# Grouped-query attention heads: the keys' low parts laid down twice, so that both score passes have 128 rows

## The chip, the core and the metric

The kernel runs on one core of a Trainium2 chip. The metric is the device time of one execution in microseconds (us). Five engines work side by side, each through its own queue in order: PE (TensorE, matrix products; the loading of its weights is shown apart as PEld), DVE (VectorE), ACT (ScalarE), POOL (GpSimd) and SP, which here issues transfers. An engine that needs another's result waits on a semaphore.

## What is computed

Two transformer blocks in float32 follow each other. The first has retention, neighbourhood attention, memory attention and a mixture of experts. The second has two layers over 512 latent tokens and 256 context tokens; each layer has three kinds of attention heads, side by side, and a feed-forward part. Cut to the heads that the change touches:

```python
q_g = _rope_2(_rms(gq.reshape(B, T, GQA_HEADS, GQA_DIM), g_gqa_q), rope_large)      # 8 heads of 64
k_g = _rope_2(_rms(gk.reshape(B, T, GQA_KV_HEADS, GQA_DIM), g_gqa_k), rope_large)   # 2 groups of keys
...
k_all = jnp.concatenate([k, kc], axis=2)          # 512 latent and 256 context keys
s = jnp.einsum('bhgqd,bhkd->bhgqk', q, k).astype(jnp.float32) * scale
p = jax.nn.softmax(s, axis=-1)
o = jnp.einsum('bhgqk,bhkd->bhgqd', p, v)
```

In layer 0 the context's 256 tokens are queries too, over the context's keys alone; in layer 1 only the 512 latents are.

## The kernel before, in words

PE takes its operands as float32r, a shortened float32. To keep the accuracy, a value is split in two such parts, high and low (`hi`, `lo`), and a product of two values is made of several products of parts that PE adds up in PSUM.

`attention` (L1759) makes a list of 20 units for a layer, one for each head or half head: 4 latent heads (`mla`), 8 differential ones (`diff`), 8 grouped-query ones (`gqa`, L1823; two groups of keys with four heads each). A unit has a preparation, a generator whose steps are run one at a time, and returns a list of passes: queries, keys, and the number of rows (features on partitions) that the product sums over.

- `mla` has three passes of 96 rows: high by high, high by low, low by high.
- `diff` lays its parts of 32 features one above the other and has one pass of 96 rows.
- `gqa` has queries of 128 rows, 64 high features above 64 low ones (`q1`). Its first pass takes them against `T1`, the high parts of the keys laid down twice (128 rows); the second takes the 64 high rows of the queries against `T2`, the low parts of the keys (64 rows). For the first head of a group the keys are prepared: `gk1` is written on DVE (L1830), `gk2` is the remainder, on POOL (L1831); both are turned on PE, six tiles of tokens each (`to_T`, L129), and copied from PSUM by ACT (L1734).

`pipeline` (L1867) runs the units one behind the other. While unit u's probabilities are turned (`turned`, PE at L131 into `tp`, then split in two parts by ACT, DVE and POOL: L1940 to L1942, L91, L92) and multiplied by the values (`products`, L1957, up to five tiles of keys later), unit u+1's scores are made (`scores`), and unit u+2 is prepared. For each tile of 128 queries `scores` runs the passes over 512 keys and then over 256 (`mms`, L1899):

```python
for j, (q, k, rows) in enumerate(passes):
    nc.tensor.matmul(p, q[:rows, qs], k[:rows, a:b], start=j == 0, stop=j == len(passes) - 1)
```

DVE takes the maximum of each row (L1905), ACT the exponential (L1908). There are two buffers in PSUM for scores (`sn`), three for turned tiles (`tp`). In layer 0 a head has four tiles of queries and then one step for the two context tiles, over 256 keys (L1913, L1919); in layer 1 it has four tiles.

What the differential heads still need, a norm over their outputs, stands behind the pipeline in the code (L1855 to L1860), but depends on their outputs alone; a scheduler orders each engine's work by what is ready and by its own estimates, and puts it among DVE's work of the grouped-query heads.

Of the kernel before, what the change touches and what calls it, by code (L numbers as in the profile page):

```python
# [8 lines left out]
F = mybir.dt.float32  # L9
# [14 lines left out]
# columns of the vector pack, in blocks of 128 features  # L24
# [8 lines left out]
# groups of 256 columns of the second block's input projection: name, first column  # L33
# [4 lines left out]
class Kern:  # L38
# [15 lines left out]
    def W(self, ap, n=2048, k=None, steps=1, pin=False, eng=None):  # L54
        """Weight chunk [128, n] of float32 from DRAM as an exact pair of float32r tiles."""
        key = ap.tensor.name, ap.offset
        if key in self.early:
            return self.early.pop(key)
        return self.pair(self.raw(ap, n), n, k, steps, pin, eng)

    def ahead(self, *chunks):
        """Loads weight chunks (name, index, k) before their use; W finds them then."""
# [10 lines left out]
    def pair(self, raw, n=2048, k=None, steps=1, pin=False, eng=None):  # L73
        """pin: not before what the engines have to do first, though it may seem ready."""
# [12 lines left out]
    def split(self, hi, lo, src, scale=None, bias=None):  # L87
        """hi + lo = src (times scale), both float32r."""
# [15 lines left out]
    def psum(self, mm, big=0, words=1024, own=()):  # L104
        """Banks of PSUM: mm of one bank, big of several."""
# [16 lines left out]
    def rows6(self, name, dtype=F):  # L122
        """[128, 6, 1024]: six tiles of rows, or what else takes their place."""
        return self.yp.tile([128, 6, 1024], dtype, name=name, tag="rows", bufs=1)
# [12 lines left out]
    def bcast_rows(self, ap, n, parts=128):  # L137
        """DRAM row of n elements seen by all partitions."""
        return bass.AP(tensor=ap.tensor, offset=ap.offset, ap=[[0, parts], [1, n]])

    def rinv(self, ss, n, count, eps, name):
        """1/sqrt(ss/count + eps) for a [128, n] tile: a first guess from the bits of the float, three Newton steps.
        With -r for the guess, (v r^2 - 3) r is 2 of the next one, and so on: -1, 2, -16, 8192 of them; v is 8192^2 of its own."""
# [33 lines left out]
    def transpose_rows(self, rows, nt, dst, evac):  # L177
        """rows: list of [128, 1024] tiles; evac(kt, t0, n, psum [128, n*128])."""
# [25 lines left out]
    # =====================================================================  # L204
# [30 lines left out]
    def b1_norm(self):  # L235
        """Loads the rows and the first weights; first_norm(t) and first_turn(t) then make the part of h of tile t."""
        nc = self.nc
        # products of nothing, that start the tensor engine's clock
# [36 lines left out]
    def first_norm(self, t):  # L275
        """Norms the row tiles from t on that share a step: 0, 1, or 2 and 3."""
# [23 lines left out]
    def w_in(self, g):  # L300
        """Columns 256*g.. of w_in, all of K."""
        return self.W(self.i["w_in"][g, 0], k=8)

    def proj_b(self, g, evac, after=lambda t: None, before=()):
        """Tokens on partitions: out[tok, 256 columns of group g]."""
# [12 lines left out]
    def proj_a(self, g, evac):  # L318
        """Columns on partitions: out[128 columns, 512 tokens]."""
# [17 lines left out]
    def retention(self):  # L337
# [6 lines left out]
        y = rp.tile([128, 4, 1024], F, name="y")              # [tok, tile, 4 heads of 256]  # L344
# [3 lines left out]
        def queries(c):  # L348
            """q and k of the heads 2c, 2c + 1: [128, hi or lo, head, tok]"""
# [34 lines left out]
        def scores(hd):  # L384
            # decay by the distance of the tokens: E[p, i - 128 j + 384] for tile j of the keys
# [15 lines left out]
        def outputs(hd):  # L401
# [4 lines left out]
            for i in range(4):  # L406
# [6 lines left out]
                # group norm over the head's 256 values  # L413
# [9 lines left out]
        # log sigmoid of the decays: min(x, 0) - log1p(exp(-|x|)), log1p by its atanh series  # L423
# [41 lines left out]
        # silu of the gate projection  # L465
# [21 lines left out]
    def branch_rows(self):  # L487
        """Where the rows of an attention branch are collected: [tok, tile, 512]."""
        return self.mix[:, 4:6].rearrange("p a (b c) -> p (a b) c", b=2)

    def branch_out(self, yT, nk, wname, gate_group, first=False, middle=lambda: None):
        """mix^T += sigmoid(gate^T) * (w^T y^T), features on partitions."""
        nc = self.nc
        nw = 2048 // nk                       # columns of w per chunk
# [1757 lines left out]
```

## Time and profile before

| | |
|---|---|
| median of three runs | 3059.8 us (3050.26 to 3065.61) |
| the profiled execution's span | 3055.9 us |
| PE busy in it | 2907.7 us (95%) |
| DVE busy | 1784.5 us (58%) |
| ACT busy | 1296.3 us (42%) |
| POOL busy | 483.3 us (16%) |
| grouped-query heads' scores, layer 0 | from 1408.2 us on |
| grouped-query heads' scores, layer 1 | up to 2589.0 us |

The profile is one execution, with the start, the length and the releaser of each instruction. PE is busy nearly throughout, but matmuls are pipelined, and the busy time of one includes what it waits for its weights. So the distance between the starts of two matmuls says more than their lengths. A line number stands for a line of the code above; a helper's line stands for all that call it.

### The profile page before, as it was taken

To read this page: it belongs to the slowest core of one execution; us is meant where nothing else is said; L and a number is where in the kernel's file an instruction comes from. 1 tells how busy PE (TensorE), PEld (TensorE's weight loads), DVE (VectorE), ACT (ScalarE), POOL (GpSimd) and SP (SyncE) were. 2 spreads that over 40 slices of the span, in tenths; PEclk is the share of its full clock that TensorE was granted. 3 is DMA by queue.
4 is the path that set the end of the run, shared out by engine and by line. 5 is a ranking of instruction groups with operands and counts; after the bars stand their busy time and mean duration, and the time that the engine had idled before them with its cause. 6 is when DMAs were issued, how large, how long until landed. Compare 5 with 4: busy or idle time off the path is not lost. (4 is left out here: it accounts for less than half of the span.)

```text
span 3055.9 us, 44719 instructions
## 1 busy us (share of the span) xinstructions
PE 2907.7 (95%) x17896; PEld 2473.1 (81%) x17896; DVE 1784.5 (58%) x3187; ACT 1296.3 (42%) x2275; POOL 483.3 (16%) x478
## 2 busy tenths in 40 slices
PE   8999999999899979899998999999898999899998
PEld 6997777679788869787688888888798776788887
DVE  6652254346688876788747242434665886644445
ACT  3232243324577754597645121211342876432222
POOL 2200010001110042255312000000310543100001
PEclk9999999999899989999999999999999999899999
DMA  5443464446799862510023121212143300322221
GB/s 197 153 140 138 143 234 152 183 155 242 267 392 378 312 225 75 179 27 19 1 90 128 59 71 54 78 48 83 62 138 98 96 20 1 125 110 96 97 97 69
DMA packets 130084, 399.78 MB, mean 131 GB/s; under 512 B 62199, under 2 KB 74887, under 8 KB 93128
## 3 DMA queue, kind: packets, MB, share of 16 engines
q1 hardware_dynamic: 116206, 350.04, 31.9%
q0 software_dynamic: 13520, 46.55, 4.6%
q8 instruction: 143, 2.34, 0.3%
q14 instruction: 71, 0.58, 0.1%
q10 hardware_dynamic: 144, 0.26, 0.0%
HBM read 356.64 MB, written 39.39 MB: 130 GB/s over the span
## 5 line engine op out<-in xcount | busy, mean ns | idle before, releaser
L82 DVE TENSOR_TENSOR wlo<-raw,whi 128x2048 fp32r<-128x2048 f32 (+2 forms) x195 | 419.3, 2153 | 280.2 <-ACT whi L81 279.7
L81 ACT ACTIVATE whi<-raw 128x2048 fp32r<-128x2048 f32 (+2 forms) x203 | 351.9, 1739 | 490.9 <-PE fd L101 132.2
L99 PE MATMUL fg<-hT,whi 128*128 128x512 f32 (+1 forms) x1120 | 389.1, 348 | 2.1 <-ACT hT L1374 2.1
L100 PE MATMUL fg<-hT,whi 128*128 128x512 f32 (+1 forms) x1120 | 389.7, 348 | 1.2 <-POOL hT L1376 1.2
L101 PE MATMUL fg<-hT,wlo 128*128 128x512 f32 (+1 forms) x1120 | 389.2, 348 | 0.0
L100 PEld LDWEIGHTS fg<-hT,whi 128*128 128x128 f32 x1120 | 213.7, 191 | 31.0 <-POOL hT L1376 1.7
L99 PEld LDWEIGHTS fg<-hT,whi 128*128 128x128 f32 x1120 | 212.1, 190 | 31.9 <-ACT hT L1374 2.5
L101 PEld LDWEIGHTS fg<-hT,wlo 128*128 128x128 f32 x1120 | 212.0, 189 | 29.0
L1942 POOL TENSOR_TENSOR pelo<-pe,pehi 128x512 fp32r<-128x512 f32 x140 | 180.7, 1292 | 233.5 <-DVE pehi L1941 227.1
L2104 DVE TENSOR_TENSOR sg<-sg,fg 128x512 f32<-128x512 f32 (+1 forms) x70 | 40.1, 572 | 295.0 <-PE fg L101 295.0
L101 PE MATMUL fd<-whi,hl 128*128 128x512 f32 x440 | 174.9, 397 | 0.0
L1905 DVE TENSOR_REDUCE smx<-sn 128x1 f32<-128x768 f32 x160 | 152.3, 952 | 38.2 <-PE sn L1899 37.7
L100 PE MATMUL fd<-wlo,hh 128*128 128x512 f32 x440 | 174.6, 397 | 0.0
L99 PE MATMUL fd<-whi,hh 128*128 128x512 f32 x440 | 174.1, 396 | 0.0
L2080 POOL TENSOR_TENSOR acc<-acc,gt 128x512 f32<-128x512 f32 x20 | 30.7, 1536 | 867.9 <-ACT sqj L164 867.9
L2075 DVE TENSOR_TENSOR acc<-acc,fd 128x512 f32<-128x512 f32 x180 | 120.7, 685 | 71.9 <-PE fd L101 71.9
L131 PE MATMUL tp<-ident,pn 128*128 128x128 f32 x960 | 151.8, 278 | 2.6 <-DVE pelo L92 1.8
L1908 ACT ACTIVATE pn<-sn,smx 128x768 f32<-128x768 f32 x160 | 143.5, 902 | 12.0 <-DVE smx L1905 6.8
L99 PE MATMUL eg<-whi,xt 128*96 128x256 f32 x512 | 146.5, 286 | 0.0
L100 PE MATMUL eg<-wlo,xt 128*96 128x256 f32 x512 | 144.6, 282 | 0.9 <-DVE wlo L82 0.9
L82 DVE TENSOR_TENSOR wlo<-rawx,whi 128x2048 fp32r<-128x2048 f32 x58 | 132.9, 2292 | 20.9 <-ACT whi L81 20.8
L101 PE MATMUL eg<-whi,xt 128*96 128x256 f32 x512 | 144.3, 282 | 0.0
(661 smaller groups left out, 7755.8 us busy)
## 6 DMA issues: line engine op xcount, KB each, us to landing
raw<-in_w_in SPq DMA_DIRECT2D x53, 1024.0 KB, 5.0
raw<-in_w_ada SPq DMA_DIRECT2D x48, 1024.0 KB, 5.1
raw<-in_f_gate SPq DMA_DIRECT2D x22, 1024.0 KB, 4.8
raw<-in_f_up SPq DMA_DIRECT2D x22, 1024.0 KB, 4.8
raw<-in_f_down SPq DMA_DIRECT2D x22, 1024.0 KB, 4.8
rawx<-in_e_gate SPq DMA_DIRECT2D x19, 1024.0 KB, 14.2
rawx<-in_e_up SPq DMA_DIRECT2D x19, 1024.0 KB, 8.9
rawx<-in_e_down SPq DMA_DIRECT2D x18, 1024.0 KB, 8.3
```

Of the source, the lines that this page charges most:

```text
L81: keep(nc.scalar.activation(hi[:, c], raw[:, c], AF.Copy))
L82: keep((eng or nc.vector).tensor_tensor(lo[:, c], raw[:, c], hi[:, c].bitcast(F), op=OP.subtract))
L99: t.matmul(ps, lh, rh, start=first, stop=False)
L100: t.matmul(ps, lh, rl, start=False, stop=False)
L101: t.matmul(ps, ll, rh, start=False, stop=last)
L131: self.nc.tensor.transpose(out, in_, self.ident[:k, :k])
L1905: nc.vector.tensor_reduce(m[:, t:t + 1], p[:, :768], axis=AX.X, op=OP.max, negate=True)
L1908: nc.scalar.activation(P[t], p[:, :768], AF.Exp, bias=m[:, t:t + 1], accum_out=su[:, t:t + 1])
L1942: nc.gpsimd.tensor_tensor(el, e, eh.bitcast(F), op=OP.subtract)
L2075: nc.vector.tensor_tensor(acc[:, t, cs], acc[:, t, cs], p, op=OP.add)
L2080: nc.gpsimd.tensor_tensor(acc[:, t, cs], acc[:, t, cs], gt[t // 4][:, cs], op=OP.mult)
L2104: nc.vector.tensor_tensor(sg, sg, pp[1], op=OP.mult)
```

## The change

The low parts of the keys are laid down twice, as the high ones already are: `gk2` becomes as wide as `gk1`, POOL makes the same subtraction a second time into its second half, the turning of `gk2` gives 128 rows and not 64, and the second pass takes all 128 rows of the queries, high and low, against it. The product of the two low parts, which was left out, comes into the scores by that.

```diff
-                k2 = ap.tile([128, 6, 64], R, name="gk2", tag="st", bufs=3)
+                k2 = ap.tile([128, 6, 2, 64], R, name="gk2", tag="st", bufs=3)
                 nc.vector.tensor_copy(k1, r[:, :, None, :].to_broadcast([128, 6, 2, 64]))
-                nc.gpsimd.tensor_tensor(k2, r, k1[:, :, 0].bitcast(F), op=OP.subtract)
+                nc.gpsimd.tensor_tensor(k2[:, :, 0], r, k1[:, :, 0].bitcast(F), op=OP.subtract)
+                nc.gpsimd.tensor_tensor(k2[:, :, 1], r, k1[:, :, 1].bitcast(F), op=OP.subtract)
                 yield
                 T1 = yield from self.to_T(ap, "gkT1", lambda t: k1[:, t].rearrange("p c d -> p (c d)"), 6, 128)
-                T2 = yield from self.to_T(ap, "gkT2", lambda t: k2[:, t], 6, 64)
+                T2 = yield from self.to_T(ap, "gkT2", lambda t: k2[:, t].rearrange("p c d -> p (c d)"), 6, 128)
...
-            return [(q1, T1, 128), (q1, T2, 64)], v
+            return [(q1, T1, 128), (q1, T2, 128)], v
```

The new file has no comments either, and its lines from L1832 on have numbers higher by one. The buffers of the tag `st` were already as large as `gk1`.

The order of the instructions on PE, DVE, ACT and SP is the same in both programs; on PE and ACT some have another size. On PE, where the keys of the first group of layer 0 are turned (`gk_14233` is `gk1`, `gk_14234` is `gk2`, `pn` the probabilities), before:

```order
L129 MATMUL tp<-identr,gk_14233 128x128 x2
L131 MATMUL tp<-ident,pn 128x128 x4
L1957 MATMUL pv<-pehi,vp 128x512
L1957 MATMUL pv<-pelo,vp 128x512
L129 MATMUL tp<-identr,gk_14234 64x128 x4
```

and after:

```order
L129 MATMUL tp<-identr,gk_14233 128x128 x2
L131 MATMUL tp<-ident,pn 128x128 x4
L1958 MATMUL pv<-pehi,vp 128x512
L1958 MATMUL pv<-pelo,vp 128x512
L129 MATMUL tp<-identr,gk_14234 128x128 x4
```

Nothing moved; the four turns give 128 rows.

On POOL, in the first group of layer 1 (`pelo` are the low parts of probabilities, `vp` the values, `gqst` the queries), before:

```order
L1721 TENSOR_TENSOR vp<-vr,vp 128x6x64
L1831 TENSOR_TENSOR gk_24040<-gkr,gk_24039 128x384
L1942 TENSOR_TENSOR pelo<-pe,pehi 128x512 x3
L1840 TENSOR_TENSOR gqst<-gqr,gqst 128x4x64
L1942 TENSOR_TENSOR pelo<-pe,pehi 128x512 x2
```

and after:

```order
L1721 TENSOR_TENSOR vp<-vr,vp 128x6x64
L1831 TENSOR_TENSOR gk_24042<-gkr,gk_24041 128x6x64
L1943 TENSOR_TENSOR pelo<-pe,pehi 128x512
L1832 TENSOR_TENSOR gk_24042<-gkr,gk_24041 128x6x64
L1943 TENSOR_TENSOR pelo<-pe,pehi 128x512 x2
L1841 TENSOR_TENSOR gqst<-gqr,gqst 128x4x64
L1943 TENSOR_TENSOR pelo<-pe,pehi 128x512 x2
```

The second subtraction stands behind one split of probabilities. In the other three groups it stands right behind the first one.

## Rows read from the trace of the kernel before

**Rows 1.** The page, its first part: busy us (share) and instructions of each engine.
```profile
PE 2907.7 (95%) x17896; PEld 2473.1 (81%) x17896; DVE 1784.5 (58%) x3187; ACT 1296.3 (42%) x2275; POOL 483.3 (16%) x478
```

**Rows 2.** Windows, differential heads, layer 0: length, busy us per engine (count), granted clock, DMA.
```profile
1359.10:1371.00 11.90, 11.06 (x80) 9.32 (x79) 11.32 (x20) 10.72 (x27) 6.40 (x6) 1.00 0.08 19
...
sum 95.60, PE 89.18 PEld 76.47 DVE 86.85 ACT 86.96 POOL 58.54; mean PE 11.15 PEld 9.56 DVE 10.86 ACT 10.87 POOL 7.32
```

**Rows 3.** Windows, grouped-query heads one, three, four and five of layer 0; sum of eight.
```profile
1408.30:1423.00 14.70, 14.70 (x81) 10.38 (x80) 11.45 (x18) 10.31 (x24) 6.14 (x5) 1.00 0.07 15
...
1438.50:1453.90 15.40, 15.35 (x84) 10.73 (x82) 13.56 (x27) 10.31 (x25) 6.29 (x5) 1.00 0.00 1
1453.90:1470.80 16.90, 16.68 (x96) 11.71 (x94) 15.27 (x30) 11.66 (x27) 7.50 (x7) 1.00 0.01 1
1470.80:1486.40 15.60, 15.49 (x84) 10.77 (x82) 12.76 (x20) 10.00 (x23) 6.82 (x6) 1.00 0.04 3
...
sum 124.30, PE 123.48 PEld 86.49 DVE 89.41 ACT 81.45 POOL 48.38; mean PE 15.44 PEld 10.81 DVE 11.18 ACT 10.18 POOL 6.05
```

**Rows 4.** Windows, grouped-query heads three, four and six of layer 1; sum of eight.
```profile
2514.10:2527.30 13.20, 12.95 (x65) 8.67 (x64) 11.05 (x25) 7.98 (x17) 4.56 (x4) 1.00 0.00 0
2527.30:2542.80 15.50, 14.92 (x82) 10.04 (x80) 13.25 (x28) 9.79 (x22) 5.44 (x5) 1.00 0.00 1
...
2554.80:2567.80 13.00, 12.68 (x66) 8.58 (x65) 7.65 (x13) 8.04 (x17) 3.82 (x3) 1.00 0.00 0
...
sum 102.70, PE 99.92 PEld 67.28 DVE 69.99 ACT 63.68 POOL 35.06; mean PE 12.49 PEld 8.41 DVE 8.75 ACT 7.96 POOL 4.38
```

**Rows 5.** The line L1899: idle us before its instructions, and how often.
```profile
  issue: 36.0, 128
```

**Rows 6.** Timeline of PE, a head of layer 0: start, us, what, count.
```profile
1423.00 1.45 PE L1899 MATMUL sn<-gkT,gqT 128*128 128x512 f32 x4
1424.38 0.66 PE L131 MATMUL tp<-ident,pn 128*128 128x128 f32 x4
1424.79 0.47 PE L1957 MATMUL pv<-pehi,vp 128*128 128x512 f32 x1
...
1434.95 1.29 PE L1899 MATMUL sn<-gkT,gqT 128*128 128x256 f32 x4
1436.18 0.66 PE L1970 MATMUL tp<-fold,oT 128*128 128x64 f32 x4
```

**Rows 7.** Timeline of PE's weight loads, a score tile; idle time and its cause in brackets.
```profile
1410.56 0.18 PEld L1899 LDWEIGHTS sn<-gkT,gqT 64*128 64x128 f32 x1 [0.24 <-issue]
1410.98 0.50 PEld L1899 LDWEIGHTS sn<-gkT,gqT 128*128 128x128 f32 x2 [0.24 <-issue]
```

**Rows 8.** Timeline of PE, a latent head of layer 0, three passes of 96 rows.
```profile
1282.29 0.60 PE L131 MATMUL tp<-ident,pn 128*128 128x128 f32 x4
1282.64 0.48 PE L1957 MATMUL pv<-pehi,vp 128*128 128x512 f32 x1
...
1283.19 0.40 PE L1899 MATMUL sn<-mhi 96*128 96x512 f32 x1
...
1283.90 0.28 PE L1899 MATMUL sn<-mhi 96*128 96x256 f32 x1
...
1284.25 0.60 PE L131 MATMUL tp<-ident,mqrow 128*96 128x128 f32 x4
```

**Rows 9.** Timeline of POOL, first group of keys, layer 0.
```profile
1387.70 0.99 POOL L1831 TENSOR_TENSOR gk<-gkr,gk 128x384 fp32r<-128x384 f32 x1
```

**Rows 10.** Timeline of PE, the same keys' low parts turned.
```profile
1399.78 0.40 PE L129 MATMUL tp<-identr,gk 128*64 128x128 f32 x4
```

**Rows 11.** Windows, behind the heads of layer 0; the granted clock is third from the end.
```profile
1548.00:1554.00 6.00, 5.69 (x26) 5.29 (x26) 1.98 (x4) 1.74 (x4) 0.00 (x0) 0.50 0.95 326
```

**Rows 12.** Timeline of PE there: matmuls of 256 columns.
```profile
1550.04 0.42 PE L100 MATMUL wo<-wlo,hT 128*128 128x256 f32 x1
1550.26 0.41 PE L99 MATMUL wo<-whi,hT 128*128 128x256 f32 x1
```

## The prediction, made before the changed kernel ran

> **What bounds the kernel now.** I read the page's engine sums first: the matmul engine (PE) is busy 95% of the span [rows 1], so time is saved where PE does less, or stands less. Its busy time counts time in which a matmul only waits for its weights, so I went on to the stretches that the change touches: per head of the second block, the busy time of each engine. In the grouped-query heads of both layers PE is at 97 to 99% of the window, and the next engine, VectorE (DVE), has 89.41 of 124.3 us and 69.99 of 102.7 [rows 3, 4]. In the differential heads just before them, whose scores take one pass, PE, DVE and ScalarE (ACT) are all at 91 to 93% [rows 2]. So here PE sets the pace; there nobody does alone.
>
> Then the line of the score matmuls, L1899: 36.0 us of idle time before its loads, 128 times, is put down to "issue": the weight loader waited for nothing that the profile shows [rows 5]. The timeline of the loader shows where: in a score tile the load of 64 rows comes 0.24 us after the load of 128 rows has ended, and the load of 128 rows after that again 0.24 us later [rows 7]. The latent and the differential heads have passes of one height, 96 rows, and no such gap stands in their timeline [rows 8].
>
> **The price of one tile.** A score tile is four matmuls: 128 rows by 512 keys, 64 by 512, 128 by 256, 64 by 256. From its start at 1423.00 to the next PE work at 1424.38 it takes 1.38 us [rows 6]. The latent heads show the same widths without a change of height: three passes of 96 rows over 512 and 256 keys, also begun behind a product with the values, run from 1283.19 to 1284.25, 1.06 us, or 0.353 a pass [rows 8]. Two passes are then 0.71. The tile gives back 1.38 - 0.71 = 0.67. The work behind it pays too: four turns take 1424.79 - 1424.38 = 0.41 behind a mixed tile [rows 6] and 1282.64 - 1282.29 = 0.35 behind even passes [rows 8]. That makes 0.73 a tile. The context's queries see 256 keys: two tiles of two passes take 1436.18 - 1434.95 = 1.23 [rows 6], against four of (1284.25 - 1283.90)/3 = 0.117 [rows 8], that is 0.47; with the 0.06 behind it, 0.82.
>
> **The sum on PE.** Layer 0 has 8 heads of 4 tiles and one such pair, layer 1 has 8 heads of 4 tiles: 64 x 0.73 + 8 x 0.82 = 46.7 + 6.6 = 53 us, or 53/288 = 0.185 for each of the 288 changes of height. A head of layer 0 gets 4 x 0.73 + 0.82 = 3.7 us shorter, one of layer 1 2.9. No matmul gets longer: the new pass streams as many columns, and 96 rows and 128 rows lie side by side in rows 8 (96-row scores, then turns of 128 rows) without a gap.
>
> **What is late next.** The order of every engine stays, but for the added subtraction, so the question is which engine can't follow. I take 3.7 or 2.9 from each head's window and hold DVE's busy time against the rest [rows 3, 4]. Layer 0: 14.7 leaves 11.0 for DVE's 11.45; 15.4 leaves 11.7 for 13.56; 16.9 leaves 13.2 for 15.27; 15.6 leaves 11.9 for 12.76. Over by 0.45 + 1.86 + 2.07 + 0.86 = 5.2 us. Layer 1: 13.2 leaves 10.3 for 11.05, 15.5 leaves 12.6 for 13.25: over by 1.4. (In these heads the end of the differential attention, L1855 to L1860, lies on DVE between the score maxima.) A DVE that never waits would thus hold back 6.6 us. It does wait: its fullest head among the differential ones in rows 2 has 11.32 of 11.9 us, 95%. On the 53.0 + 24.3 = 77.3 us of DVE work in these six heads 5% is another 4.1. Between 6.6 and 10.7 I take 9, nearer the upper end, because that head's work is the most alike. In the other ten heads DVE has room (7.65 of the 13.0 - 2.9 = 10.1 us left in a plain head of layer 1, and ACT 8.04 [rows 4]); I put 0.2 us each, 2 in all. A differential head, with all three engines near their limit, stands 11.95 us at 11.15 of PE's work [rows 2], so some waiting there is to be expected.
>
> **What is added.** Four subtractions on POOL (two groups of keys, two layers) at 0.99 us [rows 9], 4.0 us of POOL time. POOL is busy 48.38 of 124.3 us [rows 3], and the turns of the low keys come 12 us after the subtraction (from 1387.70 to 1399.78) [rows 9, 10]. In the first group of layer 1 the second subtraction comes behind one split of probabilities; the order shows it, the trace of before can't show the wait, and the same kind of cover stands before its use. Without that cover it would be at most 4 x 0.99 us on PE. Behind it on POOL stand splits of probabilities, whose products come five tiles later. What may show is DVE: work of DVE beside POOL can be slower. That lies between 0 and 4 us. The 24 turns of the low keys load 128 columns and not 64; half of a load's 0.18 us [rows 7] is 0.09 each, so between 0, where it lies beside the turn before, and 2 us. Of both together, 0 to 6, I take 1, as the cover of 12 us is long and rows 8 show loads beside matmuls. ACT's copy has more partitions and the same columns: nothing.
>
> So 53 - 9 - 2 - 1 = 41 us. The profiled execution spans 3055.9 us and the median of the three runs is 3059.8, 3.9 more; I carry the difference: 3055.9 - 41 + 3.9 = 3019.
>
> **A rule that speaks against it.** Even passes are begun every 0.117 us at 256 keys, though each has a load of its own, and a load of 128 columns takes 0.18 us even alone [rows 7, 8]: the load lies beside the matmul before it. The Trainium skill, page "TensorE: Matmul & The Clock Gate", section "Part 3: Packing small matmuls — row/col tiling", says that a weight load overlaps matmuls in flight only when it goes to another row group. By that rule two passes of full height would have their loads bare, and the widened pass would lose what overlap it had. The trace of this case doesn't agree, for passes of 96 rows; what the rule would do here is the first rival below.
>
> **Rivals.**
> - *Nothing gained* (3060). Two passes on the same rows get no load beside a matmul, so all four loads of a tile lie bare. Then a tile is 0.71 + 4 x 0.19 = 1.47 us, today's 1.38 or more. For it: "issue" names no cause. Against it: rows 8. 3%.
> - *PE's whole 53 us* (3007, and 3003 if a switch costs a little more than I read). The DVE work over the budget slips into the heads beside, which have room: 10.1 - 7.65 = 2.4 us in a plain head of layer 1 [rows 4]. For it: the excess is small. Against it: each engine keeps its order, and PE can be two score tiles ahead at most. 20%.
> - *DVE takes over more* (3029). DVE in the six full heads reaches only the 91% of the differential stretch (86.85 of 95.6): 77.3/0.91 = 85 against the 70.7 us that PE leaves, 14 lost, and the ten others lose 0.5 each, 5, with 3 us from POOL: 53 - 22 = 31. 15%.
> - *Slower: PE's clock.* With more waiting, PE could be granted the lower level in these stretches. At a granted 0.50 (1.2 of 2.4 GHz) a matmul of 256 columns begins every 0.22 us [rows 11, 12] and not every 0.117, 1.85 times as long. After the change the two stretches last some 174 us (124.3 + 102.7 - 53); the 41 us are gone, and 15 more lost, once 56/0.85 = 66 us of them run at that level: 3075 and over. For it: the level falls right after the heads [rows 11]. Against it: 1.00 in the differential head of rows 2, where PE already stands 0.84 of 11.90 us. 2%.
>
> **How the numbers follow.** My forecast 3019 has 60%. Its own span is 3011 to 3027; the range takes in the whole gain and the heavier DVE: 3003 to 3030. "Same" is within 0.5%, 15 us, about what a measurement of this kernel can tell from no change. Faster: forecast, whole gain and heavier DVE, 95%; same: nothing gained, 3%; slower 2%.
>
> **What would show it.** Right: L1899's grouped-query matmuls have one form of 128 rows, the idle time by "issue" before their loads is gone, a tile takes 0.7 to 0.8 us, the plain heads 11.6 to 12.0 us in layer 0 and 10.0 to 10.3 in layer 1, DVE is over 90% in the third to fifth head of layer 0, and PE's idle time names DVE or ACT. Wrong: gaps of 0.24 us stay between loads of one height; or heads are as long as before with PE waiting for DVE throughout; or the granted clock in these windows falls below 1.00.

## The result, and the profile after

The median goes from 3061.66 us (four runs, 3050.26 to 3065.61) to 3020.87 us (four runs, 3012.79 to 3027.51): 40.8 us less, a ratio of 0.9881 with a 95% interval of 0.9854 to 0.9908. The forecast was 3019, the gain 41.

The page's engine sums, which answer to [rows 1]; busy us, share of the span, instructions:

```profile
PE 2854.9 (95%) x17896; PEld 2464.6 (82%) x17896; DVE 1776.4 (59%) x3187; ACT 1294.7 (43%) x2275; POOL 487.9 (16%) x482
```

PE has 52.8 us less to do and is as full as before. The heads of layer 0, third, fourth, seventh and the sum of eight, against [rows 3]; length, busy us per engine (count), granted clock, DMA:

```profile
1439.30:1453.40 14.10, 12.04 (x84) 10.33 (x83) 13.76 (x26) 10.04 (x25) 6.43 (x5) 1.00 0.00 1
1453.40:1467.80 14.40, 13.04 (x97) 11.51 (x95) 14.26 (x31) 11.51 (x28) 7.84 (x7) 1.00 0.01 2
...
1493.60:1505.70 12.10, 12.05 (x84) 10.27 (x83) 8.57 (x15) 9.81 (x24) 5.13 (x4) 1.00 0.00 0
...
sum 103.60, PE 96.42 PEld 83.01 DVE 87.16 ACT 79.89 POOL 49.81; mean PE 12.05 PEld 10.38 DVE 10.89 ACT 9.99 POOL 6.23
```

The heads of layer 1, fourth, sixth and the sum, against [rows 4]:

```profile
2494.90:2509.00 14.10, 12.55 (x83) 9.93 (x81) 13.96 (x33) 9.71 (x22) 5.65 (x6) 1.00 0.01 1
...
2518.70:2529.00 10.30, 9.98 (x66) 8.27 (x65) 7.21 (x13) 7.87 (x16) 3.86 (x3) 1.00 0.00 0
...
sum 83.10, PE 79.12 PEld 65.54 DVE 67.58 ACT 62.95 POOL 36.47; mean PE 9.89 PEld 8.19 DVE 8.45 ACT 7.87 POOL 4.56
```

The 20.7 and 19.6 us are all here. In the plain heads PE is still at 95 to 100% of the window; in the third and fourth head of layer 0 and the fourth of layer 1 DVE has taken its place (98, 99 and 99%), and PE stands 1.4 to 2.1 us. In the first and fifth head of layer 0 PE is at 89% (11.28 of 12.70 us and 12.13 of 13.60).

The weight loads of the score matmuls (L1900 now), grouped by form: the 64-row group of before, then the one group of after; what stands behind the second bar is the idle time before them and its causes:

```profile
L1899 PEld LDWEIGHTS sn<-gkT,gqT 64*128 64x128 f32 x144 | 26.3, 183 | 30.7 <-issue 20.5
```

```profile
L1900 PEld LDWEIGHTS sn<-gkT,gqT 128*128 128x128 f32 x288 | 49.3, 188 | 18.1 <-ACT pn L1909 9.5 <-ACT gqT L1734 0.3
```

The line's grouped-query matmuls, and what ended the idle time before all its instructions, against [rows 5]:

```profile
L1900 PE MATMUL sn<-gkT,gqT x288: 277/286/505, 1414.2 to 2545.1; 128*128 128x256 f32 x80, 128*128 128x512 f32 x64
...
  ACT pn L1909: 29.7, 57
```

All 288 loads have 128 rows; before, 144 of them had 64. The row "issue: 36.0, 128" has gone from the list; ACT's exponential is now first in it (the 57 times cover all heads of the block). PE in the third head of layer 0, against [rows 6]; start, us, what, count, and idle time with its cause:

```profile
1439.28 0.86 PE L1900 MATMUL sn<-gkT,gqT 128*128 128x512 f32 x4
1439.98 0.60 PE L131 MATMUL tp<-ident,pn 128*128 128x128 f32 x4
1440.33 0.48 PE L1958 MATMUL pv<-pehi,vp 128*128 128x512 f32 x1
...
1444.09 0.66 PE L131 MATMUL tp<-ident,pn 128*128 128x128 f32 x4 [1.00 <-DVE pelo L92]
...
1449.66 0.72 PE L1900 MATMUL sn<-gkT,gqT 128*128 128x256 f32 x4
1450.22 0.39 PE L1958 MATMUL pv<-pehi,vp 128*128 128x512 f32 x1
```

A tile of scores takes 0.70 us (1439.28 to 1439.98; before 1.38), the four turns behind it 0.35 (before 0.41), the context's pair 0.56 (before 1.23). And PE waits 1.00 us for a low part that DVE has not yet made.

**Length of a head in every kernel that was run**, in us, from the start of its first score matmul to that of the next head's; "all" runs from the first score matmul of the eight heads to the first turn of the merged rows behind them. Each is read from one profiled execution, so these lengths leave out what varies elsewhere in the program. The experiments ran on three chips, on which the kernel before had medians of 3055.4 us (x1 to x4), 3058.9 (x5 to x7, after_again) and 3061.3 (x8, x9); across chips the ratio is to be compared.

| kernel | L0 third | fourth | fifth | seventh | L0 all | L1 fourth | seventh | L1 all | median, us | ratio to before (95%) |
|---|---|---|---|---|---|---|---|---|---|---|
| before | 15.40 | 16.93 | 15.56 | 15.48 | 139.5 | 15.49 | 12.93 | 117.6 | 3061.7 | |
| after | 14.08 | 14.44 | 13.56 | 12.14 | 118.9 | 14.11 | 10.32 | 97.9 | 3020.9 | 0.9881 (0.9854 to 0.9908) |
| x1_two_changes | 14.04 | 15.57 | 14.48 | 13.69 | 127.6 | 14.15 | 11.53 | 106.4 | 3030.1 | 0.9910 (0.9894 to 0.9926) |
| x2_preparation_alone | 15.40 | 17.06 | 15.56 | 15.48 | 139.7 | 15.60 | 12.93 | 117.7 | 3058.1 | 1.0011 (0.9995 to 1.0026) |
| x3_end_on_pool | 14.08 | 13.00 | 19.34 | 12.14 | 122.5 | 13.11 | 10.30 | 96.5 | 3018.1 | 0.9870 (0.9850 to 0.9891) |
| x4_end_left_out | 12.58 | 13.72 | 11.68 | 12.14 | 114.7 | 12.09 | 10.31 | 95.5 | 3018.1 | 0.9881 (0.9861 to 0.9901) |
| x5_latent_64 | 14.07 | 14.44 | 13.75 | 12.14 | 119.0 | 14.10 | 10.31 | 97.9 | 3056.8 | 0.9996 (0.9977 to 1.0014) |
| x6_pool_two_buffers | 14.07 | 12.99 | 12.01 | 12.13 | 115.8 | 13.08 | 10.31 | 96.5 | 3011.5 | 0.9847 (0.9817 to 0.9876) |
| x7_high_part_on_dve | 12.88 | 14.72 | 16.76 | 12.10 | 120.6 | 13.81 | 10.31 | 97.2 | 3016.0 | 0.9867 (0.9831 to 0.9904) |
| after_again | 14.07 | 14.45 | 13.59 | 12.13 | 118.9 | 14.09 | 10.32 | 97.9 | 3018.9 | 0.9865 (0.9834 to 0.9895) |
| x8_no_pool_split | 11.82 | 14.34 | 11.82 | 11.73 | 112.8 | 12.33 | 10.27 | 94.3 | 3004.1 | 0.9828 (0.9804 to 0.9852) |
| x9_both | 11.82 | 14.32 | 11.40 | 12.00 | 112.7 | 12.32 | 10.20 | 94.2 | 3010.9 | 0.9851 (0.9827 to 0.9875) |

From before to after the heads lose 20.7 + 19.7 = 40.4 us, what the medians lose (40.8). The latent and the differential heads have the same lengths in both, each within 0.1 us. The spans of the two profiled executions differ by more, 44.9 us; that is variation elsewhere (the experiment after_again).

### The profile page after: what moved, and what is told of

The parts are those of the page before. It is cut to its first block, busy times and chain, and to the rows that moved or that the text cites. A ratio compares the mean times of both kernels' runs of the same rounds, so it can differ in the third digit from the quotient of the medians.

```text
span 3011.0 us, 44725 instructions
## 1 busy us (share of the span) xinstructions
PE 2854.9 (95%) x17896; PEld 2464.6 (82%) x17896; DVE 1776.4 (59%) x3187; ACT 1294.7 (43%) x2275; POOL 487.9 (16%) x482
## 5 line engine op out<-in xcount | busy, mean ns | idle before, releaser
L1906 DVE TENSOR_REDUCE smx<-sn 128x1 f32<-128x768 f32 x160 | 151.7, 948 | 18.9 <-PE sn L1900 18.1
L2076 DVE TENSOR_TENSOR acc<-acc,fd 128x512 f32<-128x512 f32 x180 | 120.6, 685 | 68.2 <-PE fd L101 68.2
L1909 ACT ACTIVATE pn<-sn,smx 128x768 f32<-128x768 f32 x160 | 143.9, 904 | 19.6 <-DVE smx L1906 16.2
## 6 DMA issues: line engine op xcount, KB each, us to landing
rawx<-in_e_down SPq DMA_DIRECT2D x18, 1024.0 KB, 10.7
```

Source lines behind the costliest of these rows:

```text
L1906: nc.vector.tensor_reduce(m[:, t:t + 1], p[:, :768], axis=AX.X, op=OP.max, negate=True)
L1909: nc.scalar.activation(P[t], p[:, :768], AF.Exp, bias=m[:, t:t + 1], accum_out=su[:, t:t + 1])
L2076: nc.vector.tensor_tensor(acc[:, t, cs], acc[:, t, cs], p, op=OP.add)
```

## The experiments

**Half of the changes of height.** The kernel before, where every second group of passes runs in reverse order, so that two passes of 64 rows follow each other and a tile has two changes, not four:

```diff
-                for j, (q, k, rows) in enumerate(passes):
+                turn = turn and passes[0][2] != passes[-1][2]
+                for j, (q, k, rows) in enumerate(passes[::-1] if turn else passes):
...
-                mms(p[:, 512:768], t, 512, 768)
+                mms(p[:, 512:768], t, 512, 768, turn=True)
```

> The kernel before, with one edit: over the second keys of a score tile the 64-row pass comes first, so that the two 64-row passes lie side by side and a tile has two changes of height, not four (the context pair likewise). As many 64-row matmuls as before, nothing added on any other engine. Theory (each change of height costs 0.185 us): 144 of 288 changes are gone, 26.6 us of PE, and DVE's budget is kept or nearly kept in all heads; a score tile of 1.38 us takes 1.01, the eight heads of layer 0 take 124.3 - 15 = 109 us, of layer 1 102.7 - 12 = 91, the whole 25 us less than before (ratio 0.992). Rival (a 64-row pass is slow in itself, as its load never lies beside a matmul): 64-row passes are as many, so nothing is gained: tile 1.38, ratio 1.000. Second rival (the last 13 of the 53 us were never there, a change costs 0.14): 20 us, tile 1.10.

Measured: 25.2 us less than before on the same chip (3030.1 against 3055.4); the heads lose 12.0 and 11.2 us, less than the forecast 15 and 12; the third head of layer 0, for one, loses 1.36 of the 1.8 us that its ten changes are worth. The seventh head, where PE waits for other engines at most 0.3 us, loses 1.79 us for 10 changes in layer 0 and 1.40 for 8 in layer 1: 0.179 and 0.175 a change. The weight loader in the first tile of the seventh head of layer 0:

```profile
1501.14 0.19 PEld L1900 LDWEIGHTS sn<-gkT,gqT 128*128 128x128 f32 x1
1501.70 0.29 PEld L1900 LDWEIGHTS sn<-gkT,gqT 64*128 64x128 f32 x2 [0.36 <-issue]
1502.24 0.19 PEld L1900 LDWEIGHTS sn<-gkT,gqT 128*128 128x128 f32 x1 [0.25 <-issue]
1502.37 0.46 PEld L131 LDWEIGHTS tp<-ident,pn 128*128 128x128 f32 x4
```

The idle time by "issue" stands where the height changes, and only there: the second load of 64 rows follows the first without one. So the price is one of the change, not of the pass of 64 rows. The same passes, with the same work, were half as dear in another order.

**The wider low parts without the wider pass.**

```diff
-            return [(q1, T1, 128), (q1, T2, 128)], v
+            return [(q1, T1, 128), (q1, T2, 64)], v
```

> The changed kernel's preparation with the passes of before: the low parts are laid down twice and turned to 128 rows, but the second pass takes only the first 64. It measures what the change adds by itself. Theory: 1 us, bounds 0 to 6: heads of layer 0 at 124 to 126 us, of layer 1 at 103 to 104, ratio 1.000 to 1.002. Rival (the 12 us between PE's 53 and the 41 found are the price of the added work on POOL and beside it on DVE): 8 to 12 us, ratio 1.003 to 1.004, seen in the heads in which the keys are prepared (seven and eight of the differential, two and three of the grouped-query ones).

Measured: the heads are 0.23 us longer than before (0.14 + 0.09, all of it in the fourth head of each layer, where the second group's keys are prepared), and the differential heads, where the first group's are, have the lengths of before, each within 0.1 us; the ratio of the medians is 1.0011, and its interval takes in 1. The added subtractions and wider turns cost next to nothing.

**The end of the differential attention, left out or moved.** Between the score maxima of the grouped-query heads DVE also runs L1856 to L1861. x4 is the changed kernel without these lines; x3 has two of them on POOL:

```diff
-            nc.vector.tensor_tensor(y, y, r[:, t, :, None].to_broadcast([128, 4, 64]), op=OP.mult)
-            nc.vector.tensor_tensor(y, y, gd[:, None, :].to_broadcast([128, 4, 64]), op=OP.mult)
+            nc.gpsimd.tensor_tensor(y, y, r[:, t, :, None].to_broadcast([128, 4, 64]), op=OP.mult)
+            nc.gpsimd.tensor_tensor(y, y, gd[:, None, :].to_broadcast([128, 4, 64]), op=OP.mult)
```

> The changed kernel without the end of the differential attention (L1856 to L1861: the norm over the heads' outputs and its gain are left out of the computation). Theory: all of DVE's excess in the heads is gone; plain heads took 12.1 us in layer 0 and 10.3 in layer 1, so layer 0 takes 8 x 12.1 + 1 = 98 us (103.6 with it), layer 1 8 x 10.1 = 81 (83.1), together 7 to 8 us: this is what DVE's excess was worth. Rival (two score buffers and ACT's exponentials are what hold PE): 0 to 2 us.

> The changed kernel, with the two multiplications per tile that end the differential attention (L1860, L1861) on POOL and not on DVE. Theory (DVE held back the heads three to five of layer 0 and four of layer 1): with 8.7 us less on DVE in layer 0 and 4.7 in layer 1 these heads come down, layer 0 from 103.6 to 99 us, layer 1 from 83.1 to 81, the whole 5 to 7 us below the changed kernel (ratio 0.986); part is given back since DVE's casts beside POOL are slower. Rival (PE waits for the score buffers whatever DVE has to do, two buffers being too few): heads as long as in the changed kernel, 0 us. Second rival (POOL is now late, and products wait for its splits): some us longer.

x4 measured: 118.9 - 114.7 = 4.2 and 97.9 - 95.5 = 2.4 us, 6.6 together, nearly all in the heads where these operations lie (0.36 us in the one behind them in layer 1). That is what the end costs in the heads once PE is faster. The medians don't show it: 3018.1 us is the same ratio to before as the changed kernel's, 0.9881. Two profiled executions that agree in the stretch that varies by itself (the experiment after_again, 815.5 and 815.7 us) do: x4's spans 5.0 us less than after_again's, 3015.5 against 3020.5. Even so, 210.2 us are left for all heads, where 257.1 less the forecast's 53 would be 204.

x3 measured: the second and fourth head of layer 0 and the fourth of layer 1 are 0.7, 1.4 and 1.0 us shorter, but the fifth head of layer 0 takes 19.34 us and eats it up, so that the forecast 5 to 7 us aren't there. The timeline of that head shows a new wait; POOL, DVE, ACT and PE in turn:

```profile
1465.86 0.57 POOL L1765 DMA_DIRECT2D gdiff<-in_g_diff  x1 [0.29 <-POOL yB L1861]
...
1469.06 1.83 DVE L1856 TENSOR_SCALAR gdiff<-gdiff 128x64 f32<-128x64 f32 x1 [5.36 <-DMA gdiff<-in_g_diff]
...
1472.13 0.90 ACT L1909 ACTIVATE pn<-sn,smx 128x768 f32<-128x768 f32 x1 [6.51 <-DVE smx L1906]
...
1473.17 1.22 PE L1900 MATMUL sn<-gkT,gqT 128*128 128x512 f32 x2 [4.90 <-ACT pn L1909]
```

Layer 1's load of the gain has one buffer (`bufs=1`) and waits for layer 0's last use of it, which now ends on POOL. The load is issued at 1465.86, and DVE, which works in order, stands 5.36 us before the scaling of that gain (L1856), which nobody needs until layer 1; behind it stands the maximum that PE's next scores wait for. With PE standing, the granted clock falls too, to 0.83 in the mean of 1464 to 1484 us. So I gave the gain a second buffer.

**Two buffers for the gain.** x3, and

```diff
-        gd = self.small.tile([128, 64], F, name="gdiff", bufs=1)
+        gd = self.small.tile([128, 64], F, name="gdiff", bufs=2)
```

> After the change, with the twelve multiplications a layer that end the differential attention (L1860, L1861) on POOL instead of DVE, as in x3_end_on_pool, and two buffers for the gain they use (L1764), so that layer 1's load of it need not wait for layer 0's last use. Theory (in x3 the fifth head of layer 0 lost its 5 us to that late load, through one scaling of the gain queued on DVE ahead of a score maximum): that head goes from 19.3 us back to 12 to 13.5, layer 0's grouped-query heads to 114 to 117 us together (x3 122.5, after the change 118.9), layer 1's stay at 96.5, and the kernel is 4 to 7 us under the one after the change, about 3015. Rival (the fifth head was long because POOL itself, with 12 more multiplications, is late with its parts of the probabilities): it stays at 17 us or more, and the total within 2 us of x3.

Measured (the multiplications are twelve in layer 0 and eight in layer 1, which has four tiles): the fifth head goes from 19.34 to 12.01 us, the heads to 115.8 and 96.5 us, 4.5 less than after the change; 3011.5 us in the median against 3018.9 for after_again on the same chip. The cause of x3's long head is settled.

**A change of height in other heads.** The changed kernel, with a third latent pass of 64 rows:

```diff
-        return [(hi[0], hi[1], 96), (hi[0], lo[1], 96), (lo[0], hi[1], 96)], v
+        return [(hi[0], hi[1], 96), (hi[0], lo[1], 96), (lo[0], hi[1], 64)], v
```

> After the change, but the third of the three passes of the latent heads' scores takes 64 of its 96 rows (32 rows of that product are left out, so the time is of a kernel that computes less). The rows of the grouped-query heads stay at 128. Theory (what the change took away is a price for each change of height between neighbouring passes, about 0.18 us, and not something of the grouped-query heads): 96, 96, 64, 96, 96, 64 and then a turn of 128 rows are 4 changes in each of 36 tiles of scores, 144 in all, up to 26 us more, all of it inside the latent heads; 12 to 26, since parts of these heads wait for other engines and can take some of it up. The grouped-query heads stay at 118.9 and 97.9 us. Rival (a pass of 64 rows is dear only where its operands are those of the grouped-query heads, or a change from 96 to 64 rows costs nothing): the same time as after the change, or less, within 3 us.

Measured: 37.8 us more than after_again, more than the theory's upper end, with *less* arithmetic. It lies where it was forecast: the four latent heads take 19.6 us more in layer 0 and 18.7 in layer 1. Where PE's clock is granted in full, the theory's price is right. A tile in the third latent head of layer 0, begun behind a product with the values as the one in [rows 8]:

```profile
1305.45 0.40 PE L1900 MATMUL sn<-mhi 96*128 96x512 f32 x1
1305.69 0.39 PE L1900 MATMUL sn<-mlo,mhi 96*128 96x512 f32 x1
1306.01 0.50 PE L1900 MATMUL sn<-mhi,mlo 64*128 64x512 f32 x1
1306.44 0.38 PE L1900 MATMUL sn<-mhi 96*128 96x256 f32 x1
1306.66 0.28 PE L1900 MATMUL sn<-mlo,mhi 96*128 96x256 f32 x1
1306.87 0.39 PE L1900 MATMUL sn<-mhi,mlo 64*128 64x256 f32 x1
1307.18 0.64 PE L131 MATMUL tp<-ident,mqrow 128*96 128x128 f32 x4
```

1.73 us, where [rows 8] have 1.06: 0.67 for four changes, 0.168 each. The fourth latent head, at full clock in both kernels, takes 17.74 us and not 14.07: 3.67 for 20 changes, 0.184. So neither the grouped-query operands nor a height of 128 matter: 96 to 64 costs as much.

The rest is the clock. Windows of x5 in the first, second and third latent head of layer 0, and one of after_again in the second; the granted clock is third from the end:

```profile
1262.50:1266.00 3.50, 3.48 (x11) 1.82 (x11) 0.96 (x1) 0.45 (x1) 0.58 (x1) 0.94 0.59 79
...
1272.00:1280.00 8.00, 8.00 (x26) 5.51 (x26) 3.76 (x7) 3.11 (x7) 0.99 (x1) 0.50 0.42 100
...
1286.00:1292.00 6.00, 6.00 (x17) 3.65 (x17) 1.99 (x4) 1.64 (x5) 1.26 (x1) 0.50 0.00 0
...
1304.00:1310.00 6.00, 6.00 (x31) 3.96 (x30) 4.70 (x9) 5.42 (x10) 3.95 (x4) 1.00 0.01 3
```

```profile
1275.50:1280.00 4.50, 4.50 (x29) 3.83 (x29) 3.94 (x9) 4.05 (x11) 2.29 (x2) 1.00 0.35 86
```

In both kernels the clock falls to about 0.50 (1.2 of 2.4 GHz) near 1266 us. In after_again it falls in a wait of PE for a transfer, 3.14 us long, that ends at 1267.70. In x5 the fall comes before such a wait: the mean from 1262.50 to 1266.00 is already 0.94, with PE counted as busy for 3.48 of 3.50 us, and PE's wait, 1.39 us, ends at 1268.01. With even passes the clock is back at 1.00 by 1275.5. With changes of height it stays at 0.50 beyond 1292, although the profile counts PE as busy for all of it: 6.00 of 6.00 us with 17 matmuls, against 31 at full clock. The second latent head takes 22.46 us and not 11.12; in layer 1 it is 21.92 and 11.36. No other of the twelve profiled executions stays at 0.50 for over 7 us at a time in its latent heads; x5 does in both layers, for 34 and 31 us. So here the edit costs the clock as well. Whether it is the changes themselves, the smaller height or the longer distances between matmuls that holds the clock down was not tried.

**ACT's share in the plain heads.** A plain head of the changed kernel still loses some tenths. The weight loader and ACT in the seventh head of layer 0:

```profile
1496.19 0.90 ACT L1909 ACTIVATE pn<-sn,smx 128x768 f32<-128x768 f32 x1 [0.71 <-DVE smx L1906]
...
1497.24 0.76 PEld L1900 LDWEIGHTS sn<-gkT,gqT 128*128 128x128 f32 x4 [0.44 <-ACT pn L1909]
...
1499.09 0.75 PEld L1900 LDWEIGHTS sn<-gkT,gqT 128*128 128x128 f32 x4 [0.27 <-ACT pn L1909]
```

To see whether ACT's load is the cause, x7 is x6 with one high part of seven taken from ACT:

```diff
+                    elif u > 12 and k == 3:
+                        nc.vector.tensor_copy(eh, p)
+                        nc.vector.tensor_tensor(el, p, eh.bitcast(F), op=OP.subtract)
```

> x6_pool_two_buffers, and in each grouped-query head but the first of a layer one of the seven tiles of turned probabilities gets its high part from DVE instead of ACT (a copy of 128 by 512 out of PSUM, about 0.6 us less for ACT, as much more for DVE). Theory (what the plain heads still lose, 12.14 and 10.32 us against 11.8 and 10.0 of PE's work, is PE waiting for ACT's exponential to free a score buffer): the sixth and seventh heads become 0.1 to 0.3 us shorter, 11.9 to 12.0 in layer 0 and 10.1 to 10.2 in layer 1, some 2 to 3 us in all. Rival (the exponential waits for DVE's maximum, so that DVE's extra work makes it worse): these heads grow by 0.1 to 0.5 us, and the total by 2 to 6.

Measured: neither. The seventh heads stay (12.13 to 12.10, 10.31 to 10.31), and so does the sixth of layer 1 (10.31 to 10.29), so ACT's load is not what these waits hang on; the rows above have them behind the chain from score to maximum to exponential. The sixth of layer 0 is 0.42 us shorter (12.14 to 11.72), but it has 74 matmuls where x6 has 84, and the fifth 90 where x6 has 82, so it says nothing of ACT. The heads take 5.6 us more than in x6, inside the rival's 2 to 6 but not for its reason: 4.75 of them lie in the fifth head of layer 0 (16.76 us). The scheduler put all twelve multiplications on POOL in one bunch there, from 1467.8 to 1476.1 us; the window (17 operations on POOL), and PE's waits in it:

```profile
1467.60:1484.40 16.80, 15.14 (x90) 12.79 (x88) 11.62 (x20) 10.52 (x24) 14.42 (x17) 0.87 0.01 1
```

```profile
1477.41 0.38 PE L1961 MATMUL pv<-pelo,vp 128*128 128x256 f32 x1 [0.59 <-POOL pelo L1943]
...
1479.80 0.69 PE L1961 MATMUL pv<-pelo,vp 128*128 128x512 f32 x1 [0.80 <-POOL pelo L1943]
```

POOL is busy 14.42 of 16.8 us, PE waits for its low parts, and the clock goes down to 0.87 in the mean; the eight matmuls that came over from the sixth head are in it too. That is also x6's weak place: it rests on POOL having room.

**DVE beside POOL.** The forecast took DVE's busy time for work. The timeline of DVE and POOL in the third head of layer 0, after the change, speaks against that:

```profile
1446.33 1.29 POOL L1943 TENSOR_TENSOR pelo<-pe,pehi 128x512 fp32r<-128x512 f32 x1
1446.39 1.26 DVE L149 TENSOR_SCALAR dif_v<-diff_ss 128x24 f32<-128x24 f32 x1
1447.69 0.18 DVE L150 TENSOR_SCALAR dif_y<-dif_v 128x24 int32<-128x24 int32 x1
...
1449.74 1.29 POOL L1943 TENSOR_TENSOR pelo<-pe,pehi 128x512 fp32r<-128x512 f32 x1 [2.12 <-DVE dif_y L151]
1449.78 1.29 DVE L157 TENSOR_TENSOR dif_t<-dif_y 128x24 f32<-128x24 f32 x1
1451.10 0.18 DVE L158 TENSOR_TENSOR dif_t<-dif_t,dif_v 128x24 f32<-128x24 f32 x1
```

An operation on 24 elements a partition takes 0.18 us, and 1.26 and 1.29 when it starts just behind one of POOL's, until that ends. The Trainium skill, page "Trainium Architecture — The Big Picture", section "What this means for kernel authors", says that DVE and GpSimd share a pair of ports into SBUF under an exclusive lock, so that one waits while the other has it; these rows agree. They do not say it of every DVE operation. The casts of probabilities and the reciprocals of the grouped-query heads of layer 0, shortest, median and longest in ns:

```profile
L1942 DVE CAST pehi<-pe x33: 385/426/1562, 1414.3 to 1517.2; 128x512 fp32r<-128x512 f32 x33
```

```profile
L1922 DVE RECIPROCAL srec<-ssum x8: 176/191/195, 1426.4 to 1518.0; 128x6 f32<-128x6 f32 x8
```

The cast, out of and into SBUF, can take almost four times as long. The reciprocal never does, though the one at 1481.69 begins with 1.17 us of a POOL operation still to run; nor does the score maximum out of PSUM (L1906, 0.94 to 0.96 us). To test what the standing still is worth, x8 takes POOL's subtractions of probabilities away in the grouped-query heads:

```diff
-                    if self.SPLITS[6 if t0 else k]:
+                    if u < 12 and self.SPLITS[6 if t0 else k]:
```

> After the change, but in the grouped-query heads all seven tiles of turned probabilities are split the second way: ACT takes the high part straight from PSUM and DVE the low part (0.68 us), where four of the seven now go by a copy on ACT, a rounding on DVE (0.42 us, or 0.8 in the median when POOL works beside it) and a subtraction on POOL (1.29 us). DVE thus computes a little more, POOL much less. Theory (part of DVE's excess in the heads that also end the differential attention is time in which DVE's work stands still beside POOL's: an operation on 24 elements takes 1.26 and 1.29 us there and 0.18 elsewhere): the third head of layer 0 goes from 14.1 to 12.0 to 13.0 us, the fourth from 14.4 to 13.0 to 14.0, the fourth of layer 1 from 14.1 to 12.5 to 13.5, 3 to 5 us in all. Rival (only DVE's own operations count, and a tile of turns now holds its place in PSUM until DVE has read it): these heads stay or grow, by up to 0.26 us for each of four tiles, and the plain heads, 12.1 and 10.3 us now, grow by 0.2 to 0.5: 3 to 8 us more in all.

> The edits of x6_pool_two_buffers and x8_no_pool_split together: POOL has the twelve multiplications a layer that end the differential attention, and no subtraction of probabilities in the grouped-query heads. Theory: the gains add up where they lie in different heads (x6's in the fourth and fifth, x8's in the third), so that the grouped-query heads come to 111 to 114 us in layer 0 and 94 to 96 in layer 1, against 115.8 and 96.5 in x6, and the kernel to some 3008. Rival (as for x8): 3 to 8 us slower than x6, about 3015 to 3020.

x8 measured: the third head goes to 11.82 us, the fourth of layer 1 to 12.33, all heads to 112.8 and 94.3: 9.7 us less, twice the theory's upper end, and the plain heads of layer 0 gain too (the seventh 0.41). The rival falls. The fourth head of layer 0 hardly changes (14.34 us), but the border between heads has moved: in x8's order it has 103 matmuls and the third 79, after the change 97 and 84. The two together go from 28.52 to 26.16 us, inside the theory's 25 to 27, and PE has no wait left in them. What is left of POOL's work in these heads shows the same pattern, on another line:

```profile
1460.96 1.00 POOL L1841 TENSOR_TENSOR gqst<-gqr,gqst 128x384 fp32r<-128x384 f32 x1 [3.63 <-DVE gqst L1840]
1461.01 0.99 DVE L159 SCALAR_TENSOR_TENSOR dif_y<-dif_t,dif_y 128x24 f32<-128x24 f32 x1
1462.04 0.18 DVE L157 TENSOR_TENSOR dif_t<-dif_y 128x24 f32<-128x24 f32 x1
```

x8 also shortens the way from turned tile to product, by POOL's 1.29 us, and orders some work anew, so not all 9.7 us are shown to be DVE's standing still. One wait neither x8 nor x4 touches. Layer 0's first head is 12.7 us long in every kernel that has the wider pass; it begins with DVE work left over from the differential heads, two casts of it stretched beside POOL, and a wait of PE (after the change, DVE and then PE):

```profile
1414.33 1.24 DVE L1942 CAST pehi<-pe 128x512 fp32r<-128x512 f32 x1
...
1415.95 1.27 DVE L1942 CAST pehi<-pe 128x512 fp32r<-128x512 f32 x1
...
1418.01 0.67 DVE L92 TENSOR_TENSOR pelo<-tp,pehi 128x512 fp32r<-128x512 f32 x1
```

```profile
1418.74 0.36 PE L129 MATMUL tp<-identr,gqst 128*128 128x128 f32 x2 [1.42 <-DVE pelo L92]
```

x9 adds nothing to x8 (206.9 against 207.1 us of heads): with POOL out of DVE's way the multiplications may stay on DVE. x8 is the best version found; its heads give back 50.1 us of the 257.1.

**What varies by itself.** The changed kernel once more:

> The kernel after the change once more, as the measure for the other three on this chip. Theory: about 0.988 of the kernel before, 40.8 us less, with grouped-query heads of 118.9 and 97.9 us again; the feed-forward stage of layer 0, which took 533.3 us in the profiled execution before and 526.2 in the one after though neither its code nor its order changed, takes either of these. Rival (that stage is 7 us shorter because of the change): it takes 526 us in every execution that has the change. (Two kernels with the change, x3_end_on_pool and x4_end_left_out, already took 533.)

Measured: the same heads (118.9 and 97.9 us), and 815.5 us from the end of layer 0's attention to layer 1's first scores, where the profiled execution of after had 807.1 and that of before 816.9. Over all twelve profiled executions this stretch is either 805.6 to 810.1 us (after, x2, x5, x6, x7, x8) or 814.2 to 817.1 (before, x1, x3, x4, x9, after_again). The rival falls: x2, without the wider pass, has the short one, and after_again, with it, the long one. Most of the difference lies in the feed-forward part: from its first to its last matmul 578.7 us before, 570.4 after, 579.2 in after_again. So some 8 us between two executions of this program say nothing of an edit. What sets which of the two it is stayed open. x8's and x9's medians differ by 6.8 us though their heads agree within 0.2.

## Why the prediction was right

- **The price of a change of height: right.** Forecast 0.185 us for each of 288; measured 0.179 and 0.175 (x1, plain heads), 0.168 and 0.184 (x5). A tile was to take 0.71 and takes 0.70; only the context's pair is longer than forecast, 0.56 and not 0.47. With 0.177 the sum on PE is 51 us, not 53; the tile, the turns behind it and the pair as they now stand would give 53 again, so the two ways to the price differ by 2 us.
- **DVE over its budget: size right, reason half right, and some luck.** Forecast 9, bounded by 6.6 and 10.7. Against before's lengths less x1's price (3.58 a head in layer 0, 2.80 in layer 1), the six heads lose 1.50, 2.26, 1.09 and 1.58 us in layer 0 (first, third, fourth, fifth) and -0.28 and 1.42 in layer 1 (third, fourth), 7.6 together. The first head has nothing of the end of the differential attention, which begins on DVE at 1446.4, in the third head; its 1.5 us are the wait shown above. That x4 gives 6.6, the very number of the lower bound, is chance: it is what leaving the end out gives back, not DVE's excess. Nearest to the forecast's picture are the third and fourth head of layer 0, with DVE at 98 and 99%; the fifth was to be over 90% and is at 88 (11.93 of 13.6). And the term was worked out as DVE's work plus 5% of waiting, while part of that busy time was no work: it lengthens beside POOL.
- **What DVE's busy time held.** It can be estimated from the traces: in the kernel before, each DVE operation of these six heads is held against the median of the same operation with no POOL instruction beside it. What it lasts longer adds up to 1.65, 2.96, 2.91 and 2.56 us in layer 0 and 1.10 and 1.65 in layer 1, 12.8 of the 77.3. The rest, 9.8, 10.6, 12.4, 10.2, 10.0 and 11.6 us, lies below what PE was to leave in every one of these heads. So by this estimate DVE's own work was nowhere over the budget. Taking work away from POOL, with somewhat more of it for DVE, gave 9.7 us.
- **0.2 us in each other head: right for the plain ones, low for some.** From 15.48 and 12.93 the measured price leaves 11.90 (20 changes) and 10.13 (16); they take 12.14 and 10.32. The forecast lengths of 11.6 to 12.0 and 10.0 to 10.3 were missed by 0.14 and 0.02. The second and eighth head of layer 0 and the first and fifth of layer 1 lose 0.46 to 0.49 each; all ten lose 3.0, not 2.
- **The added work: smaller than forecast.** 0.23 us, against 1.
- **The sum: right, with luck.** 53 - 9 - 2 - 1 = 41 was forecast; 51 - 7.6 - 3.0 = 40.4 is what the heads gave (the losses are read from the same lengths, so this sum must close, and the added work is in them). The terms were off by 2 too much for PE, 1.4 too much for DVE, 1 too little for the other heads and 1 too much for the added work beside them, and these cancel. That the medians give 40.8, so near to the heads, is luck as well, with the interval as wide as it is and some 8 us that vary by themselves.

The rivals. *Nothing gained* falls with the tile of 0.70 us: passes on the same 128 rows have their loads beside the matmul before. The rule of the Trainium skill behind that rival (page "TensorE: Matmul & The Clock Gate", "Part 3: Packing small matmuls — row/col tiling") does not hold in this trace, now for 128 rows too. *PE's whole 53 us* wasn't reached by the change; x8 comes to 50.1. *DVE takes over more* falls: the six full heads lost 7.6 us, not the 14 it needs. *Slower: PE's clock* falls for this change, whose windows all have 1.00. Where PE waits more, in the fifth head of x3 and of x7, the mean does fall (0.83 and 0.87), and in x5, the edit that brings changes of height back, the lower level lasts for 34 and 31 us on end.

## What to carry to other kernels

Count the changes of contraction height between neighbouring matmuls, not only the matmuls: here each cost about 0.18 us, and could be had back by laying the shorter operand down twice or, for half of it and with nothing added, by reversing every second group of passes (25.2 us here). Before an engine's busy time is taken for its demand, look whether its small operations have one length: DVE operations on a few elements that last as long as a neighbour's on POOL are waiting. A load into a single buffer, and whatever is queued behind its first use, hangs on the last reader of the buffer, so moving that reader to another engine moves the load.

## What the runs showed of the hardware

- A change of height costs 0.17 to 0.18 us at full clock, between 128 and 64 rows and between 96 and 64 alike; none was seen between 96 and 128: in [rows 8] the last three passes of 96 rows and the turn of 128 rows behind them begin (1284.25 - 1283.90)/3 = 0.117 us apart, the distance of even passes.
- With such changes in every tile, PE's granted clock stayed at 0.50 from 1272 to 1292 us and beyond, while its rows count it as busy throughout; with even passes in the same place it was back at 1.00 within 10 us (x5 and after_again). It need not be so: in the kernel before, the grouped-query heads had as many changes and 1.00, and x5's own third latent head has them and 1.00 from 1304 to 1310. What makes the difference is open.
- A DVE operation on 24 elements a partition, out of and into SBUF, lasts 0.18 us alone and 0.99 to 1.29 when it starts just behind a POOL operation of that length. A reciprocal on 6 elements isn't held (0.18 to 0.20), nor is the row maximum out of PSUM (0.94 to 0.96).
